# Two exponentials moved from GpSimd to ScalarE, and the z weights of an SSD mixer loaded in two groups instead of three

## The chip, the cores and the metric

The kernel runs on one core of one Trainium2 chip. The metric is the device time of one execution in microseconds (us). Shorter is better. Five engines work side by side, each with its own queue of instructions in a fixed order: PE (TensorE, matmuls), PEld (its weight loads), DVE (VectorE), ACT (ScalarE) and POOL (GpSimd). SP (SyncE) issues most DMAs, in its own fixed order too: an entry that waits holds up those behind it.

## The reference

One layer of a hybrid encoder, for 1024 prompt tokens and 8 streams of 16 sample tokens, 1152 tokens in all, with 1024 channels. A normed input is projected by one matrix whose columns go to three mixers. Their outputs are concatenated, projected back and added to the input, and a SwiGLU block with 2816 hidden channels follows. The parts that the change touches are these:

```python
# B: Mamba-2 SSD mixer
dt = softplus(dt + dt_bias)                  # (tokens, 8 heads)
a  = -exp(a_log)                             # 8 values: "the row of A"
... s_new = exp(sum(dt*a)) * s + B^T (x * tail * dt)   # chunk by chunk
v = (y + x*d_skip) * silu(z)                 # z: 512 projected columns
out = v * rsqrt(mean(v*v)) * norm_w
# A: RG-LRU mixer
log_a = -8 * r * softplus(-lambda)           # 256 lambdas
```

## The kernel before, in words

Everything is fp32 in accuracy: a matmul operand is split into a high and a low part, and three matmuls (lines 145 to 147) make one product. The 1152 tokens are 9 tiles of 128 (tile 0 is the sample tokens), in 3 chunks of 3 tiles. The normed input of chunk c stands in the SBUF slot `hT0`, `hT1` or `hT2` as high and low parts.

The order in the source is: the norm of three chunks, the forget and query projections, `proj_vdt` (which gives `dtr`, the raw dt), the output gate `proj_og` (PSUM `ptog`, tiles `thog` and `gsog`), `ssd_steps`, the HGRN mixer `mix_c` for 9 tiles, the RG-LRU mixer `mix_a` twice, `proj_xbc`, `proj_z`, the SSD mixer `mix_b` for 9 tiles, and between these the output projection `w_out` of each chunk (PSUM `pw`). Then come the SwiGLU's two matmul stages, over half of the time.

The order of the instructions on each engine is not that of the source. The program is unrolled, and a planner (`TCARGS`: a scheduler with a simulated timeline) puts the instructions in order by priority and by the times that its cost model gives them. `feed()` and `high_priority` lift the priority of weight loads, PSUM evacuations and of `mix_b`. After the planning each engine's order is fixed, and an instruction that waits holds up all behind it on its engine.

`softplus` (line 633) works on [128, n]: it makes e = exp(-|x|) by a POOL power of the constant e (line 639; no other engine is asked for it), then a series on DVE in some 15 small instructions (lines 640 to 649). It is called with n = 2 (lambda, at the start) and with n = 72 (dt, from `ssd_steps`, tile `spt`). The row of A is made by one more POOL power of [128, 8] (line 895).

`proj_gate` (line 458) takes the token tiles given to it. For each it makes 24 matmuls of 256 columns into one of two PSUM banks of tag "a"; ACT makes the tanh (line 464), DVE the product (line 465), and a DMA writes it to DRAM. `proj_z` (line 472) calls it for chunk 0, 1 and 2 in turn, and in each for the two halves g of the 512 z columns. Each call loads its weights again: two halves of 512 KB, each split by an ACT copy (line 161) and a DVE subtraction (line 165). The staging tile `wraw` has 2 buffers, the parts `whi` and `wlo` 3 each.

What waits for z: `mix_b(t)` reads `zd[t]` back from DRAM. A slot of the input is free when the last z piece of its chunk is done. `hT0` then becomes the scratch `ws` of every second `mix_b`. `hT1` becomes `s0f`, the 2 MB SSD state of the 8 sample streams (line 941), which `mix_b(0)` works on in PSUM banks of tag "c" (`pi`, `pn`; three banks). `hT2` becomes `mT0`, the input of the first `w_out` (loaded from `mixd` by POOL's DMA queue, line 801). The tiles go in the order 1, 2, 3, then 0, 4, 5, then 6, 7, 8.

Of the kernel before, what the change touches and what calls it, by code (L numbers as in the profile page):

```python
# [15 lines left out]
AF = mybir.ActivationFunctionType  # L16
ALU = mybir.AluOpType

P = 128
D = 1024  # L20
KD = 8
NCHUNK = 3
TPC = 3
CH = TPC * P
NT = NCHUNK * TPC
# [65 lines left out]
def hybrid_step(ctx, tc, xT, xTp, vec, rows, nrow, wch, wtk0, wtk1, wout, wgate, wup, wdown,  # L91
# [3 lines left out]
    V, S, G, T = nc.vector, nc.scalar, nc.gpsimd, nc.tensor  # L95
# [12 lines left out]
    zd = dp.tile([NT, P, 512], F32, tag="zd", name="zd")  # L108
# [8 lines left out]
    cst = cp.tile([P, 4], F32, name="cst")  # L117
# [31 lines left out]
    def feed():  # L149
        return tc.high_priority(offset=PRI)  # L150
# [3 lines left out]
    def load_w(src, n, name, raw=None, ahead=True, eng=None):  # L154
        if raw is None:
            raw = wp.tile([P, 1056], F32, tag="wraw", name=f"wr_{name}", bufs=2)
        hi = wp.tile([P, 1056], F32R, tag="whi", name=f"wh_{name}")
        lo = wp.tile([P, 1056], F32R, tag="wlo", name=f"wl_{name}")
        with feed() if ahead else nullcontext():
            dma(raw[:, 0:n], src)  # L160
            S.activation(hi[:, 0:n], raw[:, 0:n], AF.Copy)
            o = name[0] == "o"
            wcount[o] += 1
            e = V
            (eng or e).tensor_tensor(lo[:, 0:n], raw[:, 0:n], hi[:, 0:n].bitcast(F32), ALU.subtract)
        return hi, lo
# [19 lines left out]
    rw = pr.tile([P, 24], F32, name="rw")  # L186
# [110 lines left out]
    def tok_piece(w, n, name, ts=range(NT)):  # L297

        for t in ts:
            hT, i = st["hT", t // TPC], t % TPC  # L300
            tg = VT[t % len(VT)] if name == "v" else "a"
            pm = bank(tg, f"pt{name}_{t}", [n])
            for k in range(KD):
                mm3(pm, (hT[:, 0, k, i * P:(i + 1) * P], hT[:, 1, k, i * P:(i + 1) * P]),
                    wk(w[k // 4], k % 4, n), k == 0, k == KD - 1)
            yield t, pm
# [151 lines left out]
    def proj_gate(w, name, dst, ts=range(NT)):  # L458

        for t, pm in tok_piece(w, 256, name, ts):  # L460
            sg = pr.tile([P, 256], F32, tag="stg", name=f"gs{name}{t}", bufs=2)
            th = pr.tile([P, 256], F32, tag="th", name=f"th{name}{t}", bufs=2)
            with feed():
                S.activation(th, pm, AF.Tanh, scale=hr1[:, t:t + 1])
                V.scalar_tensor_tensor(sg, th, 1.0, pm, ALU.add, ALU.mult)
                dma(dst[t], sg)
# [3 lines left out]
        proj_gate(w, "og", vod[:, :, 256:512])  # L470

    def proj_z():
        for c in range(NCHUNK):
            for g in range(2):
                w = [load_w(wtk1[g, h], 1024, f"t1{g}{h}{c}") for h in range(2)]
                proj_gate(w, f"z{g}", zd[:, :, g * 256:g * 256 + 256], range(c * TPC, (c + 1) * TPC))

    def proj_xbc():
        for m in range(8):
# [154 lines left out]
    def softplus(out, x, tmp, n):  # L634

        e, s, z, p = [tmp[:, j * n:(j + 1) * n] for j in range(4)]
        V.tensor_scalar(e, x, -1.0, None, ALU.mult)
        V.tensor_tensor(e, e, x, ALU.min)
        G.tensor_tensor(e, cst[:, 2:3].to_broadcast([P, n]), e, ALU.pow)
        V.tensor_scalar(s, e, 2.0, None, ALU.add)  # L640
        V.reciprocal(s, s)
        V.tensor_tensor(s, s, e, ALU.mult)
        V.tensor_tensor(z, s, s, ALU.mult)
        V.tensor_scalar(p, z, CORR[7], None, ALU.mult)
        for j in range(6, 0, -1):
            V.scalar_tensor_tensor(p, p, CORR[j], z, ALU.add, ALU.mult)
        V.scalar_tensor_tensor(p, p, 1.0, s, ALU.add, ALU.mult)
        V.tensor_scalar(e, x, 0.0, None, ALU.max)
        V.scalar_tensor_tensor(out, p, 2.0, e, ALU.mult, ALU.add)
# [3 lines left out]
    def ssd_steps():  # L653
        dt, da, acs, tot, ex, tl = [sml[:, j, :] for j in range(6)]
        softplus(dt, dtr, pr.tile([P, 576], F32, tag="W", name="spt1", bufs=2), NH)
        V.tensor_tensor(da.rearrange("p (i h) -> p i h", h=8), dt.rearrange("p (i h) -> p i h", h=8),
                        arow.unsqueeze(1).to_broadcast([P, NT, 8]), ALU.mult)
        pb = bank("d", "pacs", [2, NH])
        mm(pb[:, 0, 8:NH], cm[:, M_UP:M_UP + P], da[:, 8:NH])
        mm(pb[:, 1, 8:NH], ones, da[:, 8:NH])  # L660
        mm(pb[:, 0, 0:8], cm[:, M_US:M_US + P], da[:, 0:8])
        mm(pb[:, 1, 0:8], cm[:, M_BONE:M_BONE + P], da[:, 0:8])
        V.tensor_copy(sml[:, 2:4, :], pb)
        V.tensor_tensor(tl, tot, acs, ALU.subtract)
        S.activation(ex, acs, AF.Exp)
        S.activation(tl, tl, AF.Exp)
        S.activation(tot, tot, AF.Exp)
        pt = bank("d", "pacT", [P])
        T.transpose(pt[0:NH, :], acs, ident)
        at = pr.tile([NH, P], F32, tag="sm2", name="acT")  # L670
        V.tensor_copy(at, pt[0:NH, :])
        dma(ad, at)
        dab = pr.tile([P, NB, 8], F32, tag="oc", name="dab")
        V.tensor_tensor(dab, da[:, 0:8].unsqueeze(1).to_broadcast([P, NB, 8]),
                        seqm.unsqueeze(2).to_broadcast([P, NB, 8]), ALU.mult)
        pe = bank("d", "petb", [64])
        mm(pe, ones, dab.rearrange("p b h -> p (b h)"))
        S.activation(etb, pe.rearrange("p (b h) -> p b h", h=8), AF.Exp)
# [209 lines left out]
    nl = cp.tile([P, 4], F32, name="nl")  # L888
    V.tensor_scalar(nl[:, 0:2], vc[:, V_LAM:V_LAM + 2], -1.0, None, ALU.mult)
    softplus(nl[:, 2:4], nl[:, 0:2], spt, 2)  # L890
    sp2 = cp.tile([P, 4], F32, name="sp2")
    V.tensor_scalar(sp2[:, 0:2], nl[:, 2:4], 2.0, None, ALU.mult)
    V.tensor_scalar(sp2[:, 2:4], nl[:, 2:4], -4.0, None, ALU.mult)
    arow = cp.tile([P, 8], F32, name="arow")
    G.tensor_tensor(arow, cst[:, 2:3].to_broadcast([P, 8]), rw[:, 8:16], ALU.pow)
    V.tensor_scalar(arow, arow, -1.0, None, ALU.mult)
    Sb = pr.tile([P, 512], F32, name="Sb")
    Sc = pr.tile([P, 2, 64], F32, name="Sc")
# [33 lines left out]
    dma(o_ph, hca)  # L932
    proj_xbc()
    proj_z()
    dma(o_sca, cvs[:, 0:2])
    dma(o_scb, cvs[:, 2:10])
# [5 lines left out]
    for c in range(NCHUNK):  # L942
        ts = [POS.index(c * TPC + i) for i in range(TPC)]
# [516 lines left out]
```

## Time and profile before

| what | value |
|---|---|
| time, median of 3 runs | 1424.79 us (1423.26 to 1427.62) |
| the profiled execution's own time | 1419.54 us |
| its span | 1417.7 us |
| granted TensorE clock, mean | 0.976 of full speed |
| DMA moved | 186.91 MB, mean 132 GB/s |
| ACT table loads | 8 of 1.283 us |

All that is read from the trace comes from one profiled execution. Times in it run from the start of its span. "Busy" counts no register, semaphore or DMA-issuing instructions. A wait is time in which an engine stood idle before an instruction, put down to the last thing that this instruction needed. The granted clock is the share of full speed (2.4 GHz) that TensorE had in a stretch; the lower level is 1.2 GHz.

### The profile page before, as it was taken

The page shows a single profiled execution, that of the slowest core. Times are in us where ns is not written, and L with a number is a line of the kernel's source. Part 1 is how long each engine was busy: PE and PEld are TensorE (multiplying, and loading weights), DVE is VectorE, ACT ScalarE, POOL GpSimd, SP SyncE. Part 2 cuts the span into 40 slices and gives each one's busy share as a digit, 9 for nine tenths or more (in the row PEclk, how much of TensorE's full clock was granted, in tenths as well). Part 3 has the DMA queues.
Part 4 walks back from the last instruction along what each step waited for, and adds up shares of the span by engine and source line. Part 5 has one row for each costly group of instructions (what it writes and reads, how often), then busy time and mean ns, then how long its engine had stood idle before and what let it go on. Part 6 is the DMA issues. An engine that isn't in the chain of part 4 may idle for free.

```text
span 1417.7 us, 24313 instructions
## 1 busy us (share of the span) xinstructions
PE 1352.8 (95%) x9383; PEld 1306.4 (92%) x9383; DVE 1047.2 (74%) x1908; ACT 550.1 (39%) x976; POOL 511.5 (36%) x406
## 2 busy tenths in 40 slices
PE   8999999999999999898999999999999999999986
PEld 7899887999999898798999999999999999989985
DVE  8575687877868686799466566665666778999996
ACT  7332266444454455464312323123231453333322
POOL 4161032101015331214545345553455433452453
PEclk9999999899999999899999999999999999999998
DMA  6264121333466678560431232312323263544523
GB/s 241 78 210 131 33 96 43 107 97 101 137 213 241 213 240 276 168 193 20 151 105 57 92 119 104 104 57 92 119 101 107 86 216 110 178 145 122 170 67 135
DMA packets 96248, 186.91 MB, mean 132 GB/s; under 512 B 10300, under 2 KB 56580, under 8 KB 96004
## 3 DMA queue, kind: packets, MB, share of 16 engines
q1 hardware_dynamic: 95220, 181.42, 39.2%
q0 software_dynamic: 912, 3.93, 0.9%
q8 instruction: 74, 1.21, 0.4%
q14 instruction: 42, 0.34, 0.1%
HBM read 132.84 MB, written 52.48 MB: 131 GB/s over the span
## 4 chain that ended last, share of the span: by engine, by line
PE 64%; DVE 16%; DMA 8%; ACT 4%; issue 4%; POOL 2%; SPq 0%; DVEq 0%; POOLq 0%; ACTq 0%
PE pS_g L145 3%; PE pS_u L145 3%; PE pS_u L147 3%; PE pS_g L146 3%; PE pS_u L146 3%; PE pS_g L147 3%; PE pd L145 3%; PE pd L147 3%; PE pd L146 3%; PE pA_u L146 2%; PE pA_u L145 2%; PE pA_u L147 2%; PE pA_g L145 2%; PE pA_g L147 2%; PE pA_g L146 2%
## 5 line engine op out<-in xcount | busy, mean ns | idle before, releaser
L145 PE MATMUL pd<-e,as 128*128 128x256 f32 (+1 forms) x560 | 167.3, 301 | 8.0 <-ACT as L180 4.6
L147 PE MATMUL pd<-e,as 128*128 128x256 f32 (+1 forms) x560 | 161.8, 296 | 3.8 <-DVE as L181 3.8
L146 PE MATMUL pd<-e,as 128*128 128x256 f32 (+1 forms) x560 | 164.8, 295 | 0.0
L145 PEld LDWEIGHTS pd<-e,as 128*128 128x128 f32 x560 | 106.0, 190 | 12.3 <-ACT as L180 5.9
L181 POOL TENSOR_TENSOR al_u<-wr_u,ah_u 128x1024 fp32r<-128x1024 f32 x30 | 72.1, 2403 | 116.8 <-ACT ah_u L180 116.8
L147 PEld LDWEIGHTS pd<-e,as 128*128 128x128 f32 x560 | 104.5, 188 | 5.5 <-DVE as L181 5.5
L181 POOL TENSOR_TENSOR al_g<-wr_g,ah_g 128x1024 fp32r<-128x1024 f32 x30 | 71.9, 2399 | 93.8 <-ACT ah_g L180 93.1
L146 PEld LDWEIGHTS pd<-e,as 128*128 128x128 f32 x560 | 105.8, 189 | 0.0
L180 ACT ACTIVATE ah_g<-wr_g 128x1024 fp32r<-128x1024 f32 x30 | 31.7, 1060 | 148.1 <-PE pS_u L146 80.5
L1066 POOL TENSOR_TENSOR g<-g,pt_u 128x256 f32<-128x256 f32 (+1 forms) x80 | 77.0, 983 | 19.8 <-DVE pt_u L1062 12.6
L145 PE MATMUL pw<-mT,wh_o 128*128 128x384 f32 x192 | 68.7, 361 | 8.6 <-DVE xr L825 5.1
L145 PE MATMUL pS_g<-b,ah_g 128*128 128x256 f32 (+1 forms) x240 | 71.0, 296 | 2.0 <-ACT ah_g L180 2.0
L145 PE MATMUL pmb<-hT,wh_b 128*128 128x384 f32 x192 | 67.6, 352 | 4.0 <-DVE rawb L338 3.0
L145 PE MATMUL pA_g<-b,ah_g 128*128 128x256 f32 (+1 forms) x240 | 71.1, 296 | 0.0
L146 PE MATMUL pA_u<-b,ah_u 128*128 128x256 f32 (+1 forms) x240 | 71.0, 296 | 0.0
L145 PE MATMUL pA_u<-b,ah_u 128*128 128x256 f32 (+1 forms) x240 | 70.9, 295 | 0.0
L147 PE MATMUL pA_g<-b,al_g 128*128 128x256 f32 (+1 forms) x240 | 70.8, 295 | 0.0
L147 PE MATMUL pA_u<-b,al_u 128*128 128x256 f32 (+1 forms) x240 | 70.8, 295 | 0.0
L146 PE MATMUL pA_g<-b,ah_g 128*128 128x256 f32 (+1 forms) x240 | 70.6, 294 | 0.0
L146 PE MATMUL pS_g<-b,ah_g 128*128 128x256 f32 (+1 forms) x240 | 70.5, 294 | 0.0
L146 PE MATMUL pS_u<-b,ah_u 128*128 128x256 f32 (+1 forms) x240 | 70.4, 295 | 0.0
L145 PE MATMUL pS_u<-b,ah_u 128*128 128x320 f32 (+1 forms) x240 | 70.4, 295 | 0.0
(694 smaller groups left out, 4767.7 us busy)
## 6 DMA issues: line engine op xcount, KB each, us to landing
wr_o<-in_dram SPq DMA_DIRECT2D x24, 512.0 KB, 4.5
wr_g<-in_dram SPq DMA_DIRECT2D x20, 512.0 KB, 3.5
wr_u<-in_dram SPq DMA_DIRECT2D x20, 512.0 KB, 3.6
wd<-in_dram SPq DMA_DIRECT2D x15, 512.0 KB, 3.8
wr_t<-in_dram SPq DMA_DIRECT2D x14, 512.0 KB, 4.4
ffd<-g SPq DMA_DIRECT2D x11, 640.0 KB, 3.8
fr<-ffd SPq DMA_DIRECT2D x11, 640.0 KB, 4.7
ffd<-g SPq DMA_DIRECT2D x11, 512.0 KB, 2.6
```

The costliest lines, as they stand in the source:

```text
L145: T.matmul(out, ah, bh, start=start, stop=False)
L146: T.matmul(out, ah, bl, start=False, stop=False)
L147: T.matmul(out, al, bh, start=False, stop=stop)
L180: S.activation(dst_hi, src, AF.Copy)
L181: eng.tensor_tensor(dst_lo, src, dst_hi.bitcast(F32), ALU.subtract)
L1066: G.tensor_tensor(g, g, u, ALU.mult)
```

## The change

The power on POOL in `softplus` becomes an ACT exponential in place, with the same result; so does the power that makes the row of A. In `proj_z` the loop over three chunks becomes a loop over two groups of tiles: chunk 0 (tiles 0 to 2), then chunks 1 and 2 together (tiles 3 to 8). In each group half g = 0 is done for all its tiles and then half g = 1. So there are 4 pairs of weight loads, not 6.

```diff
     def proj_z():
-        for c in range(NCHUNK):
+        for ts in (range(TPC), range(TPC, NT)):
             for g in range(2):
-                w = [load_w(wtk1[g, h], 1024, f"t1{g}{h}{c}") for h in range(2)]
-                proj_gate(w, f"z{g}", zd[:, :, g * 256:g * 256 + 256], range(c * TPC, (c + 1) * TPC))
+                w = [load_w(wtk1[g, h], 1024, f"t1{g}{h}{ts[0]}") for h in range(2)]
+                proj_gate(w, f"z{g}", zd[:, :, g * 256:g * 256 + 256], ts)
 ...
     def softplus(out, x, tmp, n):
-        G.tensor_tensor(e, cst[:, 2:3].to_broadcast([P, n]), e, ALU.pow)
+        S.activation(e, e, AF.Exp)
 ...
-    G.tensor_tensor(arow, cst[:, 2:3].to_broadcast([P, 8]), rw[:, 8:16], ALU.pow)
+    S.activation(arow, rw[:, 8:16], AF.Exp)
```

## Rows read from the trace of the kernel before

**Rows 1.** Page: busy time of the engines; granted clock in 40 slices.

```profile
PE 1352.8 (95%) x9383; PEld 1306.4 (92%) x9383; DVE 1047.2 (74%) x1908; ACT 550.1 (39%) x976; POOL 511.5 (36%) x406
...
PEclk9999999899999999899999999999999999999998
```

**Rows 2.** Waits of PE, whole span: waiter, releaser: us in total, times, longest.

```profile
PE prr L140 <- DVE dg L214: 3.1, 1, 3.1
...
PE ptog L145 <- DVE gsog L465: 2.4, 1, 2.4
...
PE pw L145 <- ACT mT L803: 2.2, 1, 2.2
...
PE pn L140 <- DVE s0f L746: 0.9, 1, 0.9
```

**Rows 3.** Chain that ended last, 90 to 130 us: start, us, what.

```profile
94.74 11.85 POOL spt L639
```

**Rows 4.** Timeline of POOL, 94 to 110 us: start, duration, engine, line, operation.

```profile
94.73 11.84 POOL L639 TENSOR_TENSOR spt<-cst,spt 128x72 f32<-128x72 f32 x1 [8.00 <-DVE spt L638]
106.54 2.62 POOL L433 TENSOR_TENSOR bc<-bc,q 128x1152 f32<-128x1152 f32 x1
```

**Rows 5.** Timeline of DVE, the same stretch.

```profile
101.63 1.35 DVE L429 SCALAR_TENSOR_TENSOR q<-th,q 128x1152 f32<-128x1152 f32 x1
...
103.23 1.35 DVE L432 TENSOR_TENSOR ct<-ct,q 128x1152 f32<-128x1152 f32 x1
106.61 2.60 DVE L640 TENSOR_SCALAR spt<-spt 128x72 f32<-128x72 f32 x1 [2.02 <-POOL spt L639]
109.13 0.41 DVE L465 SCALAR_TENSOR_TENSOR gsog<-thog,ptog 128x256 f32<-128x256 f32 x1
```

**Rows 6.** Timeline of PE, 106.9 to 110 us; idle time and releaser in brackets.

```profile
109.59 0.39 PE L145 MATMUL ptog<-wh_t,hT 128*128 128x256 f32 x1 [2.35 <-DVE gsog L465]
```

**Rows 7.** Windows: stretch, length, busy (instructions) by engine, granted clock, DMA share, GB/s.

```profile
109.60:112.00 2.40, 2.40 (x17) 2.40 (x18) 2.16 (x10) 0.00 (x0) 0.00 (x0) 0.82 0.30 90
112.00:115.00 3.00, 3.00 (x18) 3.00 (x18) 1.97 (x8) 0.47 (x1) 0.00 (x0) 0.57 0.97 252
...
460.00:480.00 20.00, 16.93 (x78) 13.80 (x77) 11.19 (x16) 7.18 (x9) 4.77 (x7) 0.83 0.61 206
```

**Rows 8.** Groups of ACT's instructions by line: count, busy us, mean ns.

```profile
L666 ACT ACTIVATE sml<-sml 128x72 f32<-128x72 f32 x1 | 0.3, 266 | 0.0
```

**Rows 9.** Timeline of ACT, 93 to 104 us.

```profile
93.47 1.17 ACT L422 ACTIVATE bc<-bc 128x1152 f32<-128x1152 f32 x1 [1.82 <-DVE vs L453]
...
100.36 1.15 ACT L428 ACTIVATE th<-q 128x1152 f32<-128x1152 f32 x1
```

**Rows 10.** Timeline of POOL, 26 to 36 us.

```profile
26.44 1.98 POOL L895 TENSOR_TENSOR arow<-cst,rw 128x8 f32<-128x8 f32 x1
...
32.42 2.69 POOL L262 TENSOR_TENSOR xk<-xk,xk 128x1152 f32<-128x1152 f32 x1
```

**Rows 11.** Timeline of DVE, 32 to 36 us.

```profile
32.45 2.68 DVE L647 SCALAR_TENSOR_TENSOR spt<-spt 128x2 f32<-128x2 f32 x1
```

**Rows 12.** Instructions on the weight tile wr_t: duration ns min/median/max, first and last start.

```profile
L161 ACT ACTIVATE wh_t<-wr_t x16: 1043/1053/1088, 47.6 to 446.0; 128x1024 fp32r<-128x1024 f32 x14, 128x1056 fp32r<-128x1056 f32 x2
L165 DVE TENSOR_TENSOR wl_t<-wr_t,wh_t x16: 1210/1224/1731, 48.8 to 448.0; 128x1024 fp32r<-128x1024 f32 x14, 128x1056 fp32r<-128x1056 f32 x2
```

**Rows 13.** Timeline of ACT: the last two z pieces.

```profile
459.22 0.47 ACT L464 ACTIVATE thz<-ptz,hr 128x256 f32<-128x256 f32 x1 [3.62 <-PE ptz L147]
...
462.05 0.47 ACT L464 ACTIVATE thz<-ptz,hr 128x256 f32<-128x256 f32 x1 [0.35 <-PE ptz L147]
```

**Rows 14.** Timelines of SP and PE: the sample state's load, its first and last products.

```profile
422.95 0.33 SPq L941 DMA_DIRECT2D s0f<-in_dram  x1
...
434.12 0.65 PE L140 MATMUL pi<-s0f,zw 128*128 128x256 f32 x2
...
473.39 1.13 PE L140 MATMUL pn<-ws,bm 32*128 32x256 f32 x4
```

## The prediction

> **What bounds the kernel now.** First the page's busy times: PE is busy 95% of the span and no other engine comes near it [rows 1]. The change leaves every matmul as it is. So only two things can move the time: stretches in which PE stands idle, and stretches in which it runs at the lower clock (the slices of the clock row below 9, [rows 1]). The second view is therefore the waits of PE alone, over the whole span [rows 2]. Those of z's weights are not among them: no row there has `wh_t` or `wl_t` as the releaser. Four rows bear on the change: 2.4 us for `gsog`, 3.1 us for `dg` near the start, and 2.2 and 0.9 us just behind z. The third view is the chain of work that ended last, around the first of these: for 11.85 us it runs through `spt` on POOL, which is the power of the dt softplus [rows 3]. The timelines of that place tell how, and the windows the clock behind it.
>
> **The dt exponential: what goes.** POOL's power of 128x72 lasts 11.84 us, from 94.73 to 106.57 [rows 4]. DVE had put the next softplus step, L640, ahead of a gate product in its order. L640 stood still for the power until 106.61 and then took 2.60 us, up to 109.21; that is the end of POOL's next instruction, L433, 106.54 plus 2.62, to 0.05 us [rows 4, 5]. Behind it came `gsog` at 109.13, and behind that PE, which needed that PSUM bank: 2.35 us idle, from 107.24 to 109.59 [rows 5, 6]. Then the clock: 0.82 for 2.4 us and 0.57 for 3.0 us, a mix of the two levels 2.4 and 1.2 GHz, with PE busy throughout [rows 7]. At full clock that work would have taken (1 - 0.82) x 2.4 + (1 - 0.57) x 3.0 = 0.43 + 1.29 = 1.72 us less. The stall costs 2.35 + 1.72 = 4.07 us in all.
>
> **What takes its place.** An exponential of the same 128x72 on ACT stands in the trace: 266 ns [rows 8]. In this stretch ACT makes an exponential (L422) and then a tanh (L428) with no table load between them [rows 9], so the new instruction needs no load if it is put there. ACT is idle most of the time between these two, and the softplus on DVE can then run some 10 us sooner, in gaps. What is late next is L433, POOL's product: it needs L429, which ends at 101.63 + 1.35 = 102.98, and without the power it starts there and ends at 105.60. L432 on DVE, at 103.23, has two SBUF operands. What that means is shown early in the span: L647, two SBUF operands of two columns, started at 32.45 and took 2.68 us, as long as POOL's L262 from 32.42 to 35.11 [rows 10, 11]. So L432 would stand until 105.60, end at about 106.95, and `gsog` would come at 106.9 rather than 109.13. PE starts 0.46 us after it begins [rows 5, 6], at 107.36, against 107.24: 0.1 us of idle time is left. I count 4.07 - 0.1 = 4.0 us saved, all of the clock's share with it. The bounds are 0 (the planner sets the order so that another wait stands there) and 4.1. The gate work that follows fills PE without a wait until the mixers; their start hangs on the store of L433's result, which comes earlier by as much, so I carry the 4.0 us on.
>
> The Trainium skill, page "SBUF — State Buffer", section "Who interferes with whom", says that a VectorE instruction with two SBUF inputs and a GpSimd instruction that reads SBUF lock each other out, and that the loser waits for the whole of the other. The rows of L647 and L262 agree, 2.68 against 2.69 us. The power does not: L429 and L432 ran within its 11.84 us in 1.35 us each, which by the rule would have stood until 106.57. By the rule applied to the power too, taking it from POOL would also set DVE free, and nothing of the sum would change, since PE's only wait there is the one counted.
>
> **The other two exponentials.** The one of two columns and the row of A cost ACT at most 0.27 us each by the same row [rows 8], at a time when ACT splits the input. They free POOL of 1.98 us at 26.44 [rows 10]. PE's 3.1 us wait for `dg` comes after that [rows 2]: DVE stood in L647 behind POOL's L262, and L262 itself waits for ACT. Bounds: -3.1 (the wait goes) to +0.5 (two exponentials ahead of a copy that PE waits for). I take 0, since what blocks DVE there is L262, and that stays.
>
> **z.** Four weight loads of 512 KB go, and with them four ACT copies of 1.05 us and four DVE subtractions of 1.22 us [rows 12], 9.1 us of two engines. PE never waited for them [rows 2], so directly this is worth 0. What moves is the end of chunk 1. One z piece takes PE 2.83 us (462.05 - 459.22, [rows 13]). Of the 18 pieces chunk 1 was done after 12; now its second half comes behind all of the first half of chunk 2, after 15. The slot `hT1` comes free 3 pieces later, 3 x 2.83 = 8.5 us, and so the load of `s0f`, which was issued at 422.95, and its first product, at 434.12 [rows 14], come later too. SP's queue also has this load further back, behind the stores of three more pieces. z's end itself comes earlier, as PE work of `mix_b(0)` that used to lie among the z pieces now lies behind them. PE's work is the same in sum. Behind z there is a hole: 0.9 us for the sample state's chain and 2.2 us for `mT0`, which can load only when z is done [rows 2], and a clock of 0.83 over 460 to 480, which is (1 - 0.83) x 20 = 3.4 us [rows 7]; 6.5 us together. The later products of `mix_b(0)` can fill this hole, or they can be late themselves. Bounds: -6.5 to +8.5. I take 0, the nearest row being that PE is kept busy on either side.
>
> **The sum** is -4.0 + 0 + 0 = -4.0 us: 1415.5 us for the profiled execution (1419.54), whose own time is 5.25 us under the median of the runs. Set on the median, 1424.79 - 4.0 = **1420.8 us**. What a measurement can tell from no change is about 0.3%, 4.3 us, so this forecast lies just at that line.
>
> **Rivals.**
> 1. *The hole behind z closes as well.* For it: `mix_b(0)` then has 8 pairs of products and their DVE additions left at the time when PE waits for `mT0`, and ACT and DVE have 9.1 us less to do. Against: the planner orders PE by its own simulated times, and in a fixed order a product may stand behind the waiting `pw`. Up to 6.5 us more: 1424.8 - 4.0 - 6.5 = 1414.3.
> 2. *The sample state becomes the bound (slower).* The place: tile 0 of `mix_b`, whose chain from the first `s0f` product to the last `pn` took 39.3 us (434.12 to 473.39, [rows 14]). Its PSUM banks are those that tiles 4 and 5 need, and through the Sb state tiles 6 to 8 and the last `w_out` hang on them. It decides from the point at which the first product, now at 434.1 + 8.5 = 442.6 or later, comes when PE has nothing left of z and of the other tiles: six pieces behind 422.95 end at 422.95 + 17.0 = 440.0 at the earliest, other tiles' work comes on top. So it is close. At its full price, 1424.8 - 4.0 + 8.5 = 1429.3. Against: in the trace this chain was slowed by the z pieces between its own steps, which would be gone.
> 3. *The stall moves only.* The planner's order is new everywhere; with L433 earlier, DVE can be blocked ahead of `gsog` for up to 2.6 us as it was before. Then the time is about 1424.8.
>
> **How the numbers follow.** The forecast 0.42, rival 1 0.23, rival 2 0.22, rival 3 0.13. The forecast's own spread is 2 us each way and is cut by the 4.3 us line at 1420.5, so 0.20 of it counts as faster, 0.22 as no change. With rival 1: faster 0.20 + 0.23 = 0.43, and 0.02 for a start that gains by `dg`. Rival 2 at most of its price is slower: 0.21. The rest, 0.34, is no change. The range runs from 1411 (rival 1 with part of the 3.1 us of `dg`) to 1430 (rival 2 at its price), since cases of both signs count; the forecast's own is 1418.8 to 1422.8.
>
> **What would show it.** The stall: no POOL row of 11.8 us; an ACT exponential of 0.27 us between 94 and 102 us; still 8 table loads; PE's wait for `gsog` under 0.5 us and a clock of 1.00 from 107 to 115. z: 12 splits of `wr_t`, not 16; the issue of `s0f` after z piece 15; z's last tanh earlier than 462.05 less 4. Rival 1: the two waits behind z gone and a clock near 1.00 there. Rival 2: PE waits for `s0f` or `pi`, and the first `mT` of the last chunk is later than before. The forecast fails if PE's waits between 130 and 620 us change by more than 2 us in sum, either way.

## The result: slower by 0.9%

The changed kernel takes 1437.56 us (median; 1433.84 to 1439.55) against 1425.23 us for the kernel before, on the same chip: ratio 1.0091, 95% interval 1.0072 to 1.0111. The forecast was 1420.8 us, in a range of 1411 to 1430. It is wrong in sign, and the time lies outside the range.

The profiled execution of after took 1436.19 us (span 1434.3), 1.4 us under its median. That of before lies 5.69 us under its own (1425.23 less 1419.54), so this pair of traces shows 16.6 us of difference where the medians show 12.3. Times of single stages are therefore compared below with other kernels that have the same order up to that stage as well.

The page of after, busy time of the engines and granted clock in 40 slices, against [rows 1]:

```profile
PE 1356.7 (95%) x9383; PEld 1307.6 (91%) x9383; DVE 1041.2 (73%) x1904; ACT 545.3 (38%) x975; POOL 498.3 (35%) x403
...
PEclk9999999999999799999999999999999999999999
```

DVE lost 6.0 us of work, ACT 4.8, POOL 13.2, in line with the diff. PE has the same 9383 matmuls. There are still 8 table loads.

**The stall is gone, as forecast.** The timeline of after, 95 to 118 us (start, duration, engine, line, operation, in brackets the idle time before it):

```profile
95.93 0.25 ACT L639 ACTIVATE spt<-spt 128x72 f32<-128x72 f32 x1
...
97.20 0.19 DVE L640 TENSOR_SCALAR spt<-spt 128x72 f32<-128x72 f32 x1
...
103.78 1.36 DVE L429 SCALAR_TENSOR_TENSOR q<-th,q 128x1152 f32<-128x1152 f32 x1
...
105.06 0.41 DVE L465 SCALAR_TENSOR_TENSOR gsog<-thog,ptog 128x256 f32<-128x256 f32 x1
...
105.22 2.65 POOL L433 TENSOR_TENSOR bc<-bc,q 128x1152 f32<-128x1152 f32 x1 [18.10 <-DVE q L429]
...
105.39 3.70 DVE L432 TENSOR_TENSOR ct<-ct,q 128x1152 f32<-128x1152 f32 x1
```

The exponential takes 0.25 us on ACT (266 ns were taken from [rows 8]). L640 takes 0.19 us where it had stood 2.60 us [rows 5]. The planner put `gsog` ahead of L432, so the block that I expected there (L432 behind POOL's L433) happens, 3.70 us long, and PE does not wait for the `gsog` that stands next behind it (109.01). L433 ended at 107.87, and L432 ended 1.22 us later, which is about its own time without a block. The rule of the Trainium skill, page "SBUF — State Buffer", section "Who interferes with whom", says that a VectorE instruction with two SBUF inputs contends with a GpSimd instruction that reads SBUF, and that the one that issues second is blocked. L432, which came 0.17 us after L433, agrees with it by its 3.70 us.

The windows of after over the gate products (length, busy by engine, granted clock, DMA share, GB/s):

```profile
99.00:110.00 11.00, 11.00 (x92) 11.00 (x91) 10.00 (x18) 3.06 (x4) 3.97 (x3) 1.00 0.71 233
110.00:120.00 10.00, 9.01 (x78) 8.93 (x77) 3.67 (x15) 2.90 (x7) 0.00 (x0) 1.00 0.76 231
120.00:129.80 9.80, 9.80 (x86) 9.80 (x85) 1.47 (x4) 2.49 (x4) 0.00 (x0) 1.00 0.17 56
```

PE is busy for 29.81 of 30.80 us at a clock of 1.00; before, the clock there was 0.82 and 0.57 [rows 7]. The waits of PE in after (us in total, times, longest), against [rows 2]:

```profile
PE pmc L624 <- DVE oc L621: 5.3, 2, 2.7
...
PE prr L140 <- DVE arow L896: 4.5, 1, 4.5
...
PE pS_u0a L145 <- ACT ah_u0a L180: 3.9, 1, 3.9
...
PE pw L145 <- ACT mT L803: 1.5, 1, 1.5
...
PE pn L140 <- DVE s0f L746: 1.4, 2, 0.8
...
PE ptog L145 <- DVE gsog L465: 1.0, 1, 1.0
...
PE pi L140 <- DMA s0f<-in_dram: 0.7, 1, 0.7
```

The wait for `gsog` fell from 2.4 to 1.0 us and the one for `mT` from 2.2 to 1.5. The wait for `oc`, a result of the HGRN mixer, is new: before has none. No single wait explains 12 us: the loss is spread.

**Where the time went.** The HGRN mixer's results are stored by line 629, nine times (duration min/median/max, first and last start). Before:

```profile
L629 SPq DMA_DIRECT2D mixd<-mo x9: 370/371/387, 186.4 to 414.0; - x9
```

After:

```profile
L629 SPq DMA_DIRECT2D mixd<-mo x9: 370/386/432, 187.9 to 427.2; - x9
```

The first tile is 1.5 us late, the last 13.2 us. The SSD mixer follows it on the same engines. Its first transposes (line 702), before:

```profile
L702 PE MATMUL px<-cio,wb x20: 270/272/329, 395.8 to 554.7; 128*128 128x128 f32 x20
```

and after:

```profile
L702 PE MATMUL px<-cio,wb x20: 271/272/329, 411.6 to 560.9; 128*128 128x128 f32 x20
```

So this mixer starts 15.8 us late and its last tile 6.2 us. The sample state's products, `pi` (434.1 to 450.1 before, [rows 14] has the first), in after:

```profile
L140 PE MATMUL pi<-s0f,zw x32: 377/379/483, 448.2 to 464.8; 128*128 128x256 f32 x32
```

What comes last out of it is the last chunk's input of `w_out`, `mT`. The chain that ended last (start, us, what), before:

```profile
560.54 9.84 DMA mT<-mixd x2
570.40 1.07 ACT mT L803
```

and after:

```profile
568.83 9.05 DMA mT<-mixd
...
577.90 1.07 ACT mT L803
```

It comes 7.5 us later, and behind it stands all of the SwiGLU. The windows by stage: from the first z product to the first `pw`, on to the last `pw`, on to the first `pS_u`, and the rest up to the last few matmuls (length, busy of PE, PEld, DVE, ACT, POOL, clock, DMA share, GB/s). Before:

```profile
365.40:467.30 101.90, 97.03 (x726) 90.16 (x724) 76.04 (x140) 54.44 (x131) 28.32 (x27) 0.98 0.61 205
467.30:624.00 156.70, 147.61 (x828) 140.51 (x829) 118.44 (x177) 83.82 (x161) 34.82 (x31) 0.93 0.68 219
624.00:708.00 84.00, 75.71 (x542) 73.95 (x542) 64.17 (x102) 37.42 (x58) 39.10 (x21) 0.96 0.32 105
708.00:1405.30 697.30, 685.34 (x5128) 676.77 (x5127) 514.68 (x937) 208.25 (x324) 323.42 (x232) 1.00 0.35 114
```

After:

```profile
366.50:472.70 106.20, 99.60 (x735) 92.13 (x734) 71.97 (x145) 53.09 (x133) 26.34 (x28) 0.96 0.58 189
472.70:632.90 160.20, 147.88 (x831) 139.83 (x831) 118.52 (x178) 82.18 (x160) 36.49 (x31) 0.94 0.62 207
632.90:723.80 90.90, 79.68 (x544) 78.01 (x543) 65.16 (x104) 36.89 (x57) 38.40 (x21) 0.92 0.30 97
723.80:1422.20 698.40, 685.23 (x5127) 676.82 (x5126) 515.82 (x937) 208.42 (x324) 322.17 (x232) 1.00 0.35 113
```

z starts only 1.1 us later, and the last stage is 1.1 us longer. The three stages between grow by 4.3, 3.5 and 6.9 us. Length minus PE's busy time gives PE's idle time: 22.25 us before and 30.14 after, 7.9 us more. The other 6.8 us are busy time: 14 matmuls more in these stages (2110 records against 2096; they are HGRN matmuls that before has ahead of z) and a lower clock (0.92 against 0.96 in the third).

### The profile page after: what moved, and what is told of

Same layout as the page of the kernel before. It is cut to its first block, busy times and chain, and to the rows that moved or that the text cites. A ratio compares the mean times of both kernels' runs of the same rounds, so it can differ in the third digit from the quotient of the medians.

```text
span 1434.3 us, 24303 instructions
## 1 busy us (share of the span) xinstructions
PE 1356.7 (95%) x9383; PEld 1307.6 (91%) x9383; DVE 1041.2 (73%) x1904; ACT 545.3 (38%) x975; POOL 498.3 (35%) x403
## 4 chain that ended last, share of the span: by engine, by line
PE 61%; DVE 20%; DMA 9%; ACT 5%; issue 4%; POOL 1%; SPq 0%; DVEq 0%; POOLq 0%; ACTq 0%
PE pS_g L145 3%; PE pS_g L146 3%; PE pS_u L145 3%; PE pS_g L147 3%; PE pS_u L146 3%; PE pS_u L147 3%; PE pd L145 2%; PE pd L147 2%; PE pA_u L145 2%; PE pA_u L147 2%; PE pd L146 2%; PE pA_u L146 2%; PE pA_g L146 2%; PE pA_g L145 2%; PE pA_g L147 2%
## 5 line engine op out<-in xcount | busy, mean ns | idle before, releaser
L147 PE MATMUL pS_g<-b,al_g 128*128 128x256 f32 (+1 forms) x240 | 70.2, 295 | 0.0
```

The source lines that it names most:

```text
L147: T.matmul(out, al, bh, start=False, stop=stop)
```

## The experiments

Two theories stood first. A: the z part costs it all, through the sample state and the SSD tail (rival 2 of the prediction). B: the exponentials cost it all, through a new order. The kernel before was run with each set.

**e1, the z part alone** (the z edit of the change, both kinds of power left as before).

> The change's z loop alone; all three exponentials stay on POOL. Theory A (the loss of 12 us sits in z: the sample state's slot comes free three pieces later and the SSD mixer's chain is late): 1.005 to 1.009 of the kernel before, the first output-projection matmul about 5 us later and its last about 9 us later than before. Theory B (the planner's new order in the start and at the entry of SwiGLU, caused by the exponentials, is what costs): 0.998 to 1.002.

Measured: 1434.27 us, ratio 1.0069 (1.0049 to 1.0089). Of A, that the z part costs holds; that it costs all falls with the next run.

**e2, the exponentials alone** (the two exponential edits of the change, z as before).

> Both exponentials on ACT, z loop as before. Theory A: 0.997 to 1.000, since the stall of 4 us behind the power is gone and about 2 us are lost at the start. Theory B: 1.004 to 1.009. In both PE's wait for the gate product falls from 2.4 us to about 1 us, and a wait of about 4.5 us for the row broadcast stands near 37 us, as in the changed kernel.

Measured: 1434.91 us, ratio 1.0061 (1.0033 to 1.0088). Both parts cost, about 0.6 to 0.7% each, and 0.9% together. That is less than their sum, which would fit two delays of the same tail; this was not tested by itself. In e2 the last HGRN store is at 426.9 us and the first SSD transpose at 411.6, just as in after; in e1 they are at 417.4 and 400.7, and the first state product is late, at 450.8, behind a late load (438.7). In e2 that product is late too, at 447.9, but its load was issued at 416.4: there it stands behind the late mixers.

**e3, fewer loads without the new order of chunks**:

```diff
-        for c in range(NCHUNK):
-            for g in range(2):
-                w = [load_w(...) for h in range(2)]
-                proj_gate(w, ..., range(c * TPC, (c + 1) * TPC))
+        for i, (c, g) in enumerate(((0, 0), (0, 1), (1, 1), (1, 0), (2, 0), (2, 1))):
+            if i in (0, 1, 3, 5):
+                w = [load_w(...) for h in range(2)]
+            proj_gate(w, ..., range(c * TPC, (c + 1) * TPC))
```

> Exponentials as before; z in the order of chunks as before, but the two halves in the order 0 1, 1 0, 0 1, so that the weights in place are used again: 8 loads as in the change, with the slot of the sample state free after 12 pieces as before. Theory A (the slot's delay costs): 0.997 to 1.001. Theory C (fewer loads give the planner less to put between, or later prefetch of the weights behind z, and that costs): 1.004 to 1.009, like the z loop alone.

Measured: 1424.46 us, ratio 0.9989 (0.9973 to 1.0004). The 4 saved loads are worth nothing that can be told, as forecast, and they cost nothing.

**e4, the new order of pieces without fewer loads**:

```diff
+        for g, t0 in ((0, 0), (1, 0), (0, 3), (0, 6), (1, 3), (1, 6)):
+            w = [load_w(...) for h in range(2)]
+            proj_gate(w, ..., range(t0, t0 + TPC))
```

> Exponentials as before; z pieces in the changed order (chunk 0, then half 0 of chunks 1 and 2, then half 1 of both), but with 12 loads as before. Theory A: the same as the z loop alone, 1.005 to 1.009. Theory C: 0.999 to 1.001, like the kernel before.

Measured: 1436.84 us, ratio 1.0074 (1.0045 to 1.0103). The order of the pieces is the whole cost of the z part. The state's products and load in e3 (8 loads, chunk 1 done after 12 pieces):

```profile
L140 PE MATMUL pi<-s0f,zw x32: 377/379/484, 435.9 to 453.7; 128*128 128x256 f32 x32
...
L941 SPq DMA_DIRECT2D s0f<-in_dram x1: 333/333/333, 424.2 to 424.2; - x1
```

and in e1 (8 loads, chunk 1 done after 15):

```profile
L140 PE MATMUL pi<-s0f,zw x32: 377/379/796, 450.8 to 469.3; 128*128 128x256 f32 x32
...
L941 SPq DMA_DIRECT2D s0f<-in_dram x1: 376/376/376, 438.7 to 438.7; - x1
```

**e5, the row of A alone on ACT** (8 columns; both softplus powers stay on POOL):

```diff
-    G.tensor_tensor(arow, cst[:, 2:3].to_broadcast([P, 8]), rw[:, 8:16], ALU.pow)
+    S.activation(arow, rw[:, 8:16], AF.Exp)
```

> Of the exponentials only the one for the row of A (8 columns) is made by ACT; both softplus exponentials stay powers on POOL, z is as before. This one instruction is worth no more than its 1.98 us on POOL, beside other work. Order theory: what costs is that the planner, which sees other durations, writes all engines' instructions in another order from the HGRN mixer on (there tile 2 of that mixer and the first SSD tile stand some four 24-matmul products later in PE's list, and they do here too), so this kernel already loses what the three exponentials together lost: ratio 1.005 to 1.009, about 1433 us, and the first SSD tile starts near 411 us instead of 396. Rival (the three exponentials cost by themselves, on ACT's queue and by its table loads): a third or less of that, ratio 1.000 to 1.002, about 1426 us.

Measured: 1436.72 us, ratio 1.0085 (1.0065 to 1.0104). An instruction of 0.19 us, at 30.9 us of the span, costs 12.7 us (1436.72 less 1423.98 of before beside it): its own time cannot do that. The planner gave other orders, and the list on ACT shows it (lines 361 to 369 are the RG-LRU mixer's, 521 and 563 the HGRN mixer's). Around the third HGRN tile, the timeline of ACT before:

```profile
211.23 1.54 ACT L521 ACTIVATE W_b<-ldq 128x32 f32<-128x32 f32 x6 [3.23 <-PE pat L140]
...
220.46 0.69 ACT L563 ACTIVATE ke<-ldq 128x128 f32<-128x128 f32 x2
...
223.97 1.34 ACT L363 ACTIVATE a<-a,sp 128x1152 f32<-128x1152 f32 x1
...
228.03 1.26 ACT L366 ACTIVATE a<-a,cst 128x1152 f32<-128x1152 f32 x1
```

and in e5:

```profile
217.96 1.33 ACT L363 ACTIVATE a<-a,sp 128x1152 f32<-128x1152 f32 x1
...
219.20 1.53 ACT L521 ACTIVATE W_b<-ldq 128x32 f32<-128x32 f32 x6
...
222.59 1.25 ACT L366 ACTIVATE a<-a,cst 128x1152 f32<-128x1152 f32 x1
...
230.69 0.70 ACT L563 ACTIVATE ke<-ldq 128x128 f32<-128x128 f32 x2
```

Before, the HGRN tile goes first; in e5 (and in e2 and after) the RG-LRU work has been put ahead of it, and this tile and all behind it are late: it is stored at 242.8 us, against 225.9 before. The wait for `oc` stands there, 5.2 us in e5 and 5.3 in e2 and after.

**e6, all exponentials, with the HGRN tiles lifted a little in the planner; e7, that lift alone.**

```diff
     for t in range(NT):
-        mix_c(t)
+        with tc.high_priority(offset=20) if t >= 0 else nullcontext():
+            mix_c(t)
```

> All three exponentials on ACT, z as before, and the nine HGRN tiles get a priority of 20 in the planner, by which PE's list has the last HGRN tile after 75 products and the first SSD tile after 73, as before the change (79 and 77 with the exponentials alone). Order theory: the loss of 0.6% goes, and the stall of 4 us behind the dt power stays away: ratio 0.997 to 1.000, about 1422 us, first SSD tile near 393 us. Rival (the exponentials cost by themselves): ratio stays at 1.005 to 1.007, about 1433 us.

> Control: the same priority of 20 for the HGRN tiles in the kernel before, with no other edit. If the priority by itself is worth nothing, ratio 0.998 to 1.002, about 1425 us, and what the kernel with priority and exponentials gains is the stall's; if the priority itself moves the time, it is seen here, and the stall's share is the difference of the two.

Measured: e6 1430.25 us, 1.0054 (1.0033 to 1.0075), and e7 1425.7 us, 1.0010 (0.9994 to 1.0026). e6 misses the order theory's numbers: the lift of 20 mends only the end of the list. The third HGRN tile is stored at 242.9 us, much as in after (243.3; before 225.9), the last at 419.2, about halfway back, and the first SSD transpose starts at 403.0.

**e8, both causes taken away**: e3's order of z, the exponentials, and a lift of 100. It puts the third HGRN tile back (stored at 227.8 us, before 225.9) and the later ones further ahead than they were.

> Candidate for a version better than both: z halves in the order 0 1, 1 0, 0 1 (8 loads, the middle chunk's slot free after 12 pieces), three exponentials on ACT, and a priority of 100 for the HGRN tiles, which puts PE's list back to the order of before (last HGRN tile after 72 products, SSD tiles after 72 to 97). Order theory with the stall's 4 us: ratio 0.996 to 0.998, about 1420 us. Rival (exponentials cost by themselves): 1.004 to 1.007.

Measured: 1425.8 us, 1.0013 (0.9994 to 1.0032). The last HGRN store is at 398.8 us and the first state product at 434.2. The loss is gone; the expected gain did not come.

**e12, the exponentials with the lift of 100, z as before.**

> All three exponentials on ACT, z as before, priority of 100 for the HGRN tiles, which puts the last HGRN tile after 72 products and the SSD tiles after 72, 73, 78 to 97 (before: 75, and 73, 74, 78 to 97). Order theory: the loss of the exponentials is gone as in the candidate with the other order of z halves, 0.997 to 1.002, about 1424 us. If the 4 us of the stall came through to the end, 0.997; if they are given back between the og products and the start of z, 1.000. Rival (a priority does not mend it, the exponentials cost): 1.004 to 1.007.

Measured: 1424.87 us, 0.9998 (0.9980 to 1.0017). Its HGRN stores and first SSD transposes:

```profile
L629 SPq DMA_DIRECT2D mixd<-mo x9: 370/371/448, 184.1 to 398.2; - x9
```

```profile
L702 PE MATMUL px<-cio,wb x20: 270/273/421, 390.2 to 555.6; 128*128 128x128 f32 x20
```

The last SSD tile starts at 555.6, as before (554.7). e2 and e12 have the same instructions and differ in the planner's list alone, and that is 10.0 us (1434.91 less 1424.87, each beside its own runs of before, which agree to 0.3 us). So the loss of e2 lies in its order and not in the exponentials' own time. With this order nothing of the stall's 4 us is seen at the end either. One control is missing: the lift of 100 was not run on the kernel before. Its order is not before's, since it has 46 HGRN matmuls more ahead of z, and what it is worth by itself is not known.

**e9 to e11: why does the order of the z pieces cost?** With chunk 1's z later, two things are late at once: the slot for the state, and z itself. e9 makes both later still (chunks 0, 2, 1). e10 and e11 part them by giving the state the slot of chunk 2, and `mT0` that of chunk 1 (the comment behind a line says which runs have it):

```diff
-        for c in range(NCHUNK):
+        for c in (0, 2, 1):                                     # e9, e11
 ...
-        mT = slot(2 - c, f"mT{c}")
+        mT = slot((1, 2, 0)[c], f"mT{c}")                       # e10, e11
 ...
-    st["s0f"] = xp.tile([P, NB, 512], F32, tag="hT1", name="s0f")
+    st["s0f"] = xp.tile([P, NB, 512], F32, tag="hT2", name="s0f")  # e10, e11
```

> z by chunks 0, 2, 1 with 12 loads and nothing else changed: the middle chunk's z is made, and its normalised input (whose slot the sample state takes) is free, after 18 pieces instead of 12; in the change it is after 15. Dose theory (the later the middle chunk, the later the sample tile and the two behind it, and the fewer products are left to lie beside the SSD mixer's last tiles): twice the delay, about twice the 0.7% of the z part, ratio 1.010 to 1.016, about 1442 us, sample state loaded some 15 us later than with the z part alone. Rival (the order of the halves or the planner's list as such costs, and not the delay): 1.000 to 1.007.

> z by chunks 0, 1, 2 as before, but the sample state takes the slot of chunk 2 (free after 18 pieces) and the mixers' results of chunk 0 that of chunk 1: only the state is late, z is not. Slot theory (the sample tile waits for its state): ratio 1.008 to 1.016, about 1440 us. z theory (the tiles of the middle chunk wait for their own z, which comes back from DRAM): 0.998 to 1.004, about 1426 us.

> z by chunks 0, 2, 1 and the sample state in the slot of chunk 2, which is free after 12 pieces as before: the state is in time, only the z of the middle chunk is late by 6 pieces. Slot theory: ratio 0.998 to 1.004, about 1426 us. z theory: 1.008 to 1.016, about 1440 us. Both partly: near 1.006 in this run and in the one before it.

Measured: e9 1439.59 us, 1.0111 (1.0079 to 1.0143); e10 1434.89 us, 1.0071 (1.0049 to 1.0093); e11 1433.34 us, 1.0066 (1.0042 to 1.0090). The dose theory's range holds in e9: its median is the highest, though not by twice, and its interval overlaps those of e1 and e4. Between state and z the answer is both: each of them alone, 6 pieces late, costs about 0.7%, and the two together 1.1%. In e10 `mT0` also gets its slot sooner (the first `pw` starts at 449.6, before at 467.3), so the state's delay may cost more than this run shows. In e10 the load itself is late:

```profile
L140 PE MATMUL pi<-s0f,zw x32: 377/379/484, 458.9 to 479.0; 128*128 128x256 f32 x32
...
L941 SPq DMA_DIRECT2D s0f<-in_dram x1: 333/333/333, 449.5 to 449.5; - x1
```

In e11 the state is there in time, issued at 428.1, but the planner's list has the tile behind its z: its first product comes after all 84 of the 24-matmul products up to z's end, where before has it after 80. It comes late all the same:

```profile
L140 PE MATMUL pi<-s0f,zw x32: 379/379/483, 462.8 to 477.4; 128*128 128x256 f32 x32
...
L941 SPq DMA_DIRECT2D s0f<-in_dram x1: 332/332/332, 428.1 to 428.1; - x1
```

All runs side by side (times from each profiled execution, us):

| run | ratio | last HGRN store | first SSD transpose | first state product | last `pw` |
|---|---|---|---|---|---|
| before | | 414.0 | 395.8 | 434.1 | 624.0 |
| after | 1.0091 | 427.2 | 411.6 | 448.2 | 632.9 |
| e1 z alone | 1.0069 | 417.4 | 400.7 | 450.8 | 633.4 |
| e2 exponentials alone | 1.0061 | 426.9 | 411.6 | 447.9 | 635.9 |
| e3 8 loads, old order | 0.9989 | 415.3 | 396.5 | 435.9 | 626.6 |
| e4 12 loads, new order | 1.0074 | 417.7 | 401.2 | 451.2 | 635.8 |
| e5 row of A alone | 1.0085 | 430.9 | 415.5 | 451.4 | 643.7 |
| e6 exponentials, lift 20 | 1.0054 | 419.2 | 403.0 | 442.8 | 634.2 |
| e7 lift 20 alone | 1.0010 | 416.6 | 401.7 | 446.1 | 632.0 |
| e8 e3 + exponentials, lift 100 | 1.0013 | 398.8 | 391.1 | 434.2 | 629.5 |
| e9 chunk 1 last | 1.0111 | 411.5 | 395.3 | 455.7 | 632.7 |
| e10 state late | 1.0071 | 412.2 | 396.1 | 458.9 | 624.6 |
| e11 z late | 1.0066 | 419.1 | 400.8 | 462.8 | 633.2 |
| e12 exponentials, lift 100 | 0.9998 | 398.2 | 390.2 | 434.1 | 624.2 |

The kernels whose first state product is at 434 to 436 us are before, e3, e8 and e12, and none of the three loses anything. The reverse does not hold: in e7 that product is 12.0 us late, the first SSD transpose 5.9, and the time is the same, so such a delay is a mark of the cost and not the price by itself. Single executions also scatter: the profiled ones of before and e10 lie 5.7 and 6.3 us under their medians, those of e1, e4 and e5 4.7, 4.9 and 6.1 over them, so a time in the table is good to some 5 us. No kernel here is faster than before by more than can be told; e3, e7, e8 and e12 are equal to it.

## Why the prediction was wrong

The gain of 4.0 us was counted rightly for its stage and then carried to the end, where it did not arrive. And two terms that were put at 0 were losses: what the exponentials do to the planner's order (e2 lost 8.7 us, 0.0061 x 1424.87, where -4.0 was forecast), and the later end of chunk 1 in z (e1 lost 9.8 us, 0.0069 x 1424.87).

**"I count ... 4.0 us saved" was right for its stage.** Take the kernels with before's order up to z: before, e1, e3, e4 and e9 to e11. Their last `ptog` product starts at 130.9, 133.9, 133.9, 134.5, 131.6, 132.4 and 134.0 us, mean 133.0. With the dt exponential on ACT (after, e2, e6, e8, e12) it starts at 129.8, 128.6, 128.2, 129.3 and 129.9, mean 129.2: 3.9 us sooner (133.03 less 129.16). From the first `ptog` product to the last it is 34.5 us in the first set and 29.8 in the second. But in e5 it is 31.0, with the long power still on POOL: PE waits 2.3 us for `gsog` there, as long as before, but in two pieces, and the clock from 100 to 130 us is 1.00. So by this measure most of the gain, 3.5 of 4.7 us, came with e5's order alone, and the exponential's own share is not shown.

**"The gate work that follows fills PE without a wait until the mixers ... so I carry the 4.0 us on" is the step that failed first.** The first z product starts at a mean of 367.4 us in the first set (365.4, 370.3, 367.2, 369.3, 364.9, 365.7, 368.8) and 367.2 in the second (366.5, 364.9, 370.1, 367.8, 366.9): of 3.9 us, 0.1 is left (367.37 less 367.24), with a scatter of some 2 us between executions. But the second set has not done the same work by then. PE has 2163 matmuls ahead of z in the first set and in e6, 2149 in after and e2, and 2209 in e8 and e12. In after the gain is lost before z: between the gate products and z PE is idle for 9.4 us (9.8 in e2), with the new wait for `oc` in it, against 6.5 in before and 7.7 in the other six of the first set, and 14 matmuls fewer are done. In e8 and e12 it is not lost there. PE is idle for 6.2 us, and the gain stands ahead of z as 46 matmuls more. It goes behind z: from the first z product to the last `pw` PE is idle for 20.1 and 18.3 us in these two, against 14.0 in before and 13.2 in e3. With fewer matmuls left to lie beside the SSD mixer, PE stands idle for longer.

**"The other two exponentials ... I take 0"**, with bounds of -3.1 to +0.5, was worked out from durations and engines alone. The prediction says of the planner's order that it is "new everywhere", and uses it only in rival 3, as a way to lose the 4 us. The one of 8 columns costs 1.0085 by itself (e5). The step left out is that a removed POOL instruction moves the planner's simulated time, that the orders of all engines are drawn from it, and that an order can put a tile of one mixer behind a long stretch of another. That this term was missing from the sum, and from its bounds, is the larger of the two errors (12.7 us from -4.0 to +8.7): the kernels with exponentials lose 0.6 to 0.85% with the planner's new list (e2, e5) and nothing with that of a lift of 100 (e12). The reason given for the 0, that L262 "itself waits for ACT", is not in the rows either: at 32.42 it follows on POOL's own work without idle time [rows 10].

**"z ... I take 0" is the second.** "PE never waited for them [rows 2], so directly this is worth 0" was right (e3). "The slot hT1 comes free 3 pieces later, 3 x 2.83 = 8.5 us, and so the load of `s0f`" was right in kind: 14.5 us from e3 to e1 (424.2 to 438.7). Rival 2 named the place and the chain, at 8.5 us; e1 lost 9.8 us. It had a chance of 0.22, and I took the middle of two bounds in its stead. "The nearest row being that PE is kept busy on either side" was the weak reason: PE's work is the same in sum, but what is moved behind z runs at a granted clock of 0.94 and 0.92 (after, the two stages from the first `pw` on), beside a chain that decides when the last `mT` is there. Rival 2 also missed that chunk 1's z itself, not only the state, holds the tiles (e11).

**Rival 1** (the hole behind z closes too) is out: from z's start to the first `pS_u` PE is idle for 7.9 us more, not less. (Its 3.4 us for the clock also took in PE's idle time; with 16.93 us busy [rows 7] it is 2.9.)

**What was to show it** was well chosen in part. No power on POOL, an exponential of 0.25 us, 8 table loads, a clock of 1.00 and 12 splits of `wr_t` came as written. The wait for `gsog` was to be under 0.5 us and is 1.0, and z's last tanh, which was to come before 458.05, comes at 461.61. Rival 2's sign is there: PE waits for `s0f` (0.7 us), and the last chunk's `mT` is 7.5 us late. The condition on PE's waits between 130 and 620 us is met on the side of failure: the idle time from the gate products to the last `pw` grew by about 8 us.

## What to carry to other kernels

Where a planner fixes the orders, an edit near the start, however small, can be an edit of all orders: compare the lists, or price a new list by its own runs, before an instruction's own microseconds are added up. A transfer or stage that feeds the last serial chain should be judged by when that chain can start and by how much other work is left beside it, not by what it spares on engines that PE does not wait for. And a stall removed far from the end may be worth only what the next serial chain lets through: work done ahead of that chain can come back as idle time beside it (e8, e12).

## What the runs showed that I had not expected

An exponential of 128x8 on ACT in place of a POOL power of 1.98 us cost 12.7 us (e5). Priorities of 20 and 100 on the same nine tiles gave ratios of 1.0054 and 0.9998 with the same instructions. Removing the 128x72 power did not free DVE of the block behind the POOL product L433: it moved from L640 (2.60 us before, 0.19 after) to L432, which ran in 1.35 us within the power [rows 5] and takes 3.70 us now that it meets L433.
